# Two windowed attentions in a two-group encoder: a unit's transposes first, then its products with the values in one run; the sample's attention of layer 1 goes quad by quad over both halves

## The chip, the cores and the metric

The kernel runs on one core of a Trainium2 chip. The metric is the device time of one execution in microseconds (us). "Layer 0" is the even layer of the reference, "layer 1" the odd one. "Sample" is the group of 1024 tokens (letter s in names), "prompt" the group of 512 (letter p).

## The reference, cut to what matters

Two groups go through the same two layers with shared weights. Layer 0 has a dense attention and mixture B, a mixture of sliding windows at three dilations over 8 heads. Layer 1 has attention C, a neighbourhood attention on a grid 64 wide with a learned bias over 12 heads, and a Fourier mixer. Each layer is a projection in, the mixers, a gate, a projection out, a norm and a residual. Attention C, cut:

```
def row_block(args):
    r, qr = args
    r0 = jnp.clip(r - kh // 2, 0, rows - kh)
    kr = lax.dynamic_slice_in_dim(kg, r0, kh, axis=1)
    vr = lax.dynamic_slice_in_dim(vg, r0, kh, axis=1)
    bias = rpb[:, row_idx[None, :, None], col_idx[:, None, :]]
    sc = jnp.einsum('bchd,bjkhd->bhcjk', qr, kr) * scale + bias[None]
    sc = jnp.where(col_mask[None, None, :, None, :], sc, NEG_INF)
    p = jax.nn.softmax(sc.reshape(b, h, GRID_W, kh * GRID_W), axis=-1)
    return jnp.einsum('bhcjk,bjkhd->bchd', p, vr)
```

Mixture B is three such softmaxes with windows of 128, 512 and 2048 at dilations 1, 4 and 16, weighted by their sums; the kernel computes them as one softmax.

## The kernel before, in words

Linear layers run on TensorE as three products each of a high and a low part (`mm`, line 143; `tok_gemm`, `chan_gemm`). The names of their outputs tell the job: `t1v` values, `c1k`, `c1q`, `c1g` and `c1d` keys, queries and gates of layer 1, `y` the projection out. The weights come by DMA (`ws...`), are split by ScalarE (`wh...`) and by VectorE or GpSimd (`wl...`). All loads and stores are issued by one queue, that of SyncE (SP), in order; a load whose buffer is still read waits at its head, and all behind it wait too.

**Attention C** (`attn_c_unit`) works in units of one head and one half of the queries (512 of them; the prompt has one half). That makes 24 units for the sample and 12 for the prompt. A unit has four tiles of 128 queries. For each tile: scores on TensorE (`scs` or `scp`), bias and maximum on VectorE (L1096), exponential on ScalarE (L1101), division on VectorE (L1104), three transposes (two for the prompt) into one PSUM tile (`ptcs`, L147), one copy of it to SBUF (`ptccs`, L664, in turn on VectorE and ScalarE), and three (two) products with the values (`ocs`, L670). At the unit's end `fold` (L679, L680) adds the two halves of the output and a DMA stores it (`m1s`).

A product with the values (`pv2`) uses only 64 of the array's columns: `tile_position=(0, 64 * (n % 2))` puts successive products of a unit on the left and the right half by turns, and `fold` adds the halves. Each product of these numbers is two matmul instructions in the trace (288 products of `ocs` are 576 instructions).

**Mixture B** (`attn_b_pair`, `out_b`) works in pairs of heads and one half of the queries. Its scores (`sbs`, `sbp`, lines 800 and 805) use tiles of the array too: eight products of L805, each 64 rows by 32 columns, stand behind two or four of L800. `out_b` then transposes a head's probabilities into four PSUM tiles (`pt1`, `pt2`; three for the prompt), copies each (`ptc1`, `ptc2`) and multiplies with the values (`obs`, `obp`): 14 products for a head of the sample, ten for one of the prompt.

PSUM has two buffers for transposes (TB = 2), one for the output of a unit (OB = 1) and two for scores (SB = 2). The copies have four buffers (tags `pth` and `ptl`, PTB = 2 each), values five (VB = 5).

**Order.** `run` writes the jobs in a list; in layer 1 of the sample it is u0, then k, q, v for each of three quads of heads, then g0, g1, g2 and d0. Attention C of a quad is called behind the job of its values. A scheduler in the framework then decides at build time how the instructions of different calls are interleaved on each engine; on the chip each engine takes its list in order. After the last job, `s3` projects the prompt's output (`y`), and `s3_two` the sample's. Their left operand is made by `s3_operand`: for each of eight blocks two loads (`og` from `m1` and `g1`), a product with the gate (L890, on GpSimd or VectorE), a cast (`hhm`, L891, ScalarE) and a difference (`hlm`, L892, VectorE). The blocks go through three buffers (tag `sp`, SPB = 3), which the gates' outputs (`gt1d`) use as well.

Of the kernel before, what the change touches and what calls it, by code (L numbers as in the profile page):

```python
# [18 lines left out]
P = 128  # L19
D = 1024  # L20
KC = D // P
HD = 64
# [100 lines left out]
class Body:  # L123
# [537 lines left out]
    def copy_pt(self, pt, nm, w=512, rows=P):  # L661
        self.np += 1
        t = self.sb.tile([P, 512], F32, tag="pt" + "hl"[self.np % 2], name="ptc" + nm, bufs=PTB)
        (self.nc.vector.tensor_copy if self.np % PTD == 0 else self.nc.scalar.copy)(t[:rows, :w], pt[:rows, :w])  # L664
        return t

    def pv2(self, out, v, p, n):

        x = 64 * (n % 2)
        self.nc.tensor.matmul(out[x:x + HD], v, p, start=n < 2, stop=False, tile_position=(0, x), skip_group_check=True)  # L670

    def fold(self, po, nm, w=512, view=None):

# [147 lines left out]
    def out_b(self, g, h, pr, x, ev, V1, V2, nm):  # L821
        hf = g.hf
        po = self.pO(f"o{nm}")

        for gi in range(2):
            pt = self.pT(f"pt1{nm}{gi}")
            for i, (t, j) in enumerate(((0, 0), (0, 1), (1, 0), (1, 1))):
                self.tr(pt[:, i * P:(i + 1) * P], ev[2 * gi + t][:, j * P:(j + 1) * P])
            ph = self.copy_pt(pt, f"1{nm}{gi}")
            for j, t, cnt, b in ((0, 0, 1, 0), (1, 0, 2, 1), (2, 1, 1, 3)):  # L830
                t += 2 * gi
                self.pv2(po[:, t * P:(t + cnt) * P], V1[2 * gi + j], ph[:, b * P:(b + cnt) * P], j if gi == 0 else 2 + j)

        pc = po.rearrange("p (t r a) -> p r t a", t=4, r=4)
        for kt in range(hf):
            pt = self.pT(f"pt2{nm}{kt}")
            for t in range(4):
                self.tr(pt[:, t * P:(t + 1) * P], ev[t][:, 256 + kt * P:256 + (kt + 1) * P])
            p2 = self.copy_pt(pt, f"2{nm}{kt}").rearrange("p (t r a) -> p r t a", t=4, r=4)
            for r in range(4):  # L840
                self.pv2(pc[:, r], V2[r * hf + kt], p2[:, r], 2 + r)
        of = self.fold(po, nm, view=lambda v: v.rearrange("p (t r a) -> p r t a", t=4, r=4))
        self.dma(self.md[0, g.name, pr][HD * x:HD * x + HD, 512 * h:512 * h + 512], of)

# [204 lines left out]
    def attn_c_unit(self, g, h, head):  # L1049

        nc, pool = self.nc, self.sb
        n, S, nh = g.name, g.S, g.nhalf
        nrow = 12 if nh == 2 else 8
        NG = nrow // 4
# [26 lines left out]
        for kind, wo, w in ((0, 8, 24), (1, 0, 32), (2, 0, 24)):  # L1081
            b = self.l1.tile([P, nrow, w], F32, tag="bias", name=f"bi{nm}{kind}", bufs=BB)
            nc.gpsimd.tensor_add(b, T[:, :, wo:wo + w], self.mcol[:, kind, wo:wo + w].unsqueeze(1).to_broadcast([P, nrow, w]))  # L1083
            bias[kind] = b
        po = self.pO("o" + nm)
        k3 = km.rearrange("p (r c) -> p r c", c=GRID)
        for i in range(4):
            c0, c1 = max(16 * i - 8, 0), min(16 * i + 24, GRID)
            w = c1 - c0
            W, kw = nrow * w, 4 * w  # L1090
            b = bias[(0, 1, 1, 2)[i]]
            e = pool.tile([P, 1024], F32, tag="e", name=f"e{nm}{i}", bufs=EB)[:, 0:W]
            ps = self.pS(f"s{nm}{i}")[:, 0:W]
            self.qk(ps.rearrange("p (r c) -> p r c", c=w), q, slice(P * i, P * i + P), k3[:, :, c0:c1])
            m = pool.tile([P, 1], F32, tag="nmax", name=f"m{nm}{i}", bufs=4)
            nc.vector.tensor_tensor_reduce(out=e, in0=ps, in1=b.rearrange("p r w -> p (r w)"), scale=1.0,  # L1096
                                           scalar=-3.0e38, op0=ALU.add, op1=ALU.max, accum_out=m)
            ngm = pool.tile([P, 1], F32, tag="nmx2", name=f"ngm{nm}{i}", bufs=4)
# [9 lines left out]
            ph = self.copy_pt(pt, f"{nm}{i}", NG * P, kw)  # L1108
            for x in range(NG):
                self.pv2(po[:, i * P:(i + 1) * P], Vs[i][:kw, x], ph[:kw, x * P:(x + 1) * P], NG * i + x)  # L1110
        self.dma(self.md[1, n, pr][HD * hh:HD * hh + HD, 512 * h:512 * h + 512], self.fold(po, nm))


# [111 lines left out]
    def run(self):  # L1225
# [85 lines left out]
        with tc.tile_pool(name="l1", bufs=1) as self.l1:  # L1311
# [30 lines left out]
            for n, kind in enumerate(jobs):  # L1342
# [7 lines left out]
                if n == FS[1]:  # L1350
                    third(*four)
                    for q in range(3):
                        self.attn_c(gp, 0, q)
                elif kind[0] == "v":
                    self.attn_c(gs, 0, int(kind[1]))
                    if kind == "v2":
                        for q in range(3):
                            self.attn_c(gs, 1, q)
# [41 lines left out]
```

## Time and profile before

| | |
|---|---|
| median of 3 runs | 1936.8 us (1934.24 to 1936.91) |
| the profiled execution | 1936.24 us, of which span of the instructions 1934.2 us |
| busy share of the span | TensorE 96%, VectorE 62%, ScalarE 48%, GpSimd 31% |
| mean granted clock of TensorE | 0.988 |
| DMA | 333 MB, 172 GB/s |

The span runs from the first to the last instruction; the profiled execution is 2.0 us longer than its span. Times in the rows below are us from the span's start. A matmul's end is modelled, so the distance of two starts is the better measure of what one costs.

### The profile page before, as it was taken

The numbers are of one execution on the slowest core, as the hardware profiler recorded it, in microseconds if no ns is written. First come the engines' busy times: TensorE is split into PE (matmuls) and PEld (weight loads), VectorE is DVE, ScalarE is ACT, GpSimd is POOL, SyncE is SP. The second block draws the span as 40 slices with busy tenths as digits, with TensorE's granted clock in tenths as the row PEclk, the third lists the DMA queues.
The fourth block names the chain that finished last, engine by engine and source line by source line (L and its number), as shares of the span: only waits on it lengthen the run. The fifth ranks groups of instructions, "written<-read, shape, count | busy, mean of one in ns | idle before, by whom it ended". The sixth has DMA issues, their size and how long they took to land. (4 is left out here: it accounts for less than half of the span.)

```text
span 1934.2 us, 37850 instructions
## 1 busy us (share of the span) xinstructions
PE 1857.0 (96%) x13752; PEld 1614.9 (83%) x13752; DVE 1195.3 (62%) x3110; ACT 927.1 (48%) x2197; POOL 591.4 (31%) x534
## 2 busy tenths in 40 slices
PE   6999999999999999999999989799999999998998
PEld 4789768999998988889977667788887888887898
DVE  2688863254767666767765677564566544668733
ACT  3456543343356554555554555453554433445531
POOL 3631224354722121121101121353433323335310
PEclk9999999999999999999999999899999999999999
DMA  9754445467763323244344563654677664668643
GB/s 303 253 175 147 126 138 184 126 197 224 231 207 112 104 93 108 64 135 145 116 146 150 182 193 113 205 181 136 216 233 224 195 180 150 200 206 267 221 156 142
DMA packets 255353, 333.03 MB, mean 172 GB/s; under 512 B 25672, under 2 KB 172456, under 8 KB 255168
## 3 DMA queue, kind: packets, MB, share of 16 engines
q1 hardware_dynamic: 255168, 330.62, 54.4%
q8 instruction: 108, 1.77, 0.4%
q14 instruction: 77, 0.63, 0.1%
HBM read 248.68 MB, written 81.87 MB: 171 GB/s over the span
## 5 line engine op out<-in xcount | busy, mean ns | idle before, releaser
L143 PE MATMUL y<-who,hhm 128*128 128x256 f32 x768 | 219.9, 288 | 13.0 <-ACT hhm L891 13.0
L143 PE MATMUL y<-who,hlm 128*128 128x256 f32 x768 | 218.6, 288 | 2.9 <-DVE hlm L892 2.9
L143 PE MATMUL y<-wlo,hhm 128*128 128x256 f32 x768 | 218.6, 287 | 0.2 <-DVE wlo L386 0.2
L143 PEld LDWEIGHTS y<-who,hhm 128*128 128x128 f32 x768 | 148.1, 193 | 16.6 <-ACT hhm L891 14.1
L143 PEld LDWEIGHTS y<-who,hlm 128*128 128x128 f32 x768 | 147.6, 193 | 5.4 <-DVE hlm L892 3.9
L143 PEld LDWEIGHTS y<-wlo,hhm 128*128 128x128 f32 x768 | 148.2, 194 | 1.8 <-issue 1.4
L717 ACT ACTIVATE eas<-sas,nmas 128x512 f32<-128x512 f32 x128 | 86.8, 684 | 69.9 <-DVE nmas L713 69.6
L1083 POOL TENSOR_TENSOR bics<-TTcs,mkc 128x288 f32<-128x288 f32 (+1 forms) x72 | 65.5, 911 | 127.7 <-DVE mcs L1096 108.1
L654 DVE TENSOR_TENSOR ptlas<-ptas,pthas 128x512 fp32r<-128x512 f32 x128 | 85.7, 685 | 19.6 <-ACT pthas L652 18.8
L386 POOL TENSOR_TENSOR wlo<-wso,who 128x512 fp32r<-128x512 f32 x40 | 55.9, 1400 | 132.4 <-ACT who L385 106.5
L708 DVE TENSOR_REDUCE mxas<-sas 128x1 f32<-128x512 f32 x128 | 86.3, 683 | 12.7 <-PE sas L143 12.2
L652 ACT CAST pthas<-ptas 128x512 fp32r<-128x512 f32 x128 | 70.5, 590 | 29.1 <-PE ptas L147 25.7
L143 PE MATMUL t1v<-wh1v,hh 128*128 128x256 f32 x288 | 82.2, 286 | 0.0
L143 PE MATMUL t1v<-wh1v,hl 128*128 128x256 f32 x288 | 82.0, 285 | 0.0
L143 PE MATMUL t1v<-wl1v,hh 128*128 128x256 f32 x288 | 81.9, 285 | 0.0
L1101 ACT ACTIVATE ecs<-ecs,ngmcs 128x288 f32<-128x288 f32 (+1 forms) x96 | 54.8, 571 | 56.3 <-DVE ngmcs L1099 54.8
L914 ACT ACTIVATE ysq<-y 128x256 f32<-128x256 f32 x96 | 36.6, 382 | 87.7 <-PE y L143 70.6
L147 PE MATMUL ptas<-ident,eas 128*128 128x128 f32 x512 | 76.6, 273 | 0.3 <-DVE eas L725 0.3
L143 PE MATMUL oas<-pthas,Vas 128*128 128x256 f32 x256 | 68.9, 285 | 0.0
L143 PE MATMUL oas<-ptlas,Vas 128*128 128x256 f32 x256 | 68.5, 294 | 0.2 <-DVE ptlas L654 0.2
L891 ACT CAST hhm<-og 128x512 fp32r<-128x512 f32 x48 | 29.7, 619 | 75.4 <-POOL og L890 46.1
L385 ACT CAST who<-wso 128x512 fp32r<-128x512 f32 x80 | 48.7, 616 | 35.3 <-PE y L143 10.8
(628 smaller groups left out, 6317.2 us busy)
## 6 DMA issues: line engine op xcount, KB each, us to landing
wso<-w_out_ab SPq DMA_DIRECT2D x48, 256.0 KB
kcs<-k1s SPq DMA_DIRECT2D x24, 384.0 KB
wso<-w_out_cd SPq DMA_DIRECT2D x32, 256.0 KB
ws1k<-w_in_cd SPq DMA_DIRECT2D x28, 256.0 KB
wskb<-w_in_ab SPq DMA_DIRECT2D x24, 256.0 KB
wsqb<-w_in_ab SPq DMA_DIRECT2D x24, 256.0 KB
wsvb<-w_in_ab SPq DMA_DIRECT2D x24, 256.0 KB
ws1q<-w_in_cd SPq DMA_DIRECT2D x24, 256.0 KB
```

Of the source, the lines that this page charges most:

```text
L143: self.nc.tensor.matmul(out, l, r, start=start, stop=stop, skip_group_check=True)
L147: self.nc.tensor.transpose(out, in_, self.ident[:k, :k])
L385: nc.scalar.copy(hi, st)
L386: (nc.vector if c in dve else nc.gpsimd).tensor_sub(lo, st, hi)
L652: nc.scalar.copy(h[:rows, :w], pt[:rows, :w])
L654: nc.vector.tensor_sub(lo[:rows, :w], pt[:rows, :w], h[:rows, :w])
L708: nc.vector.tensor_reduce(mx[:, c:c + 1], ps, op=ALU.max, axis=AX.X, negate=True)
L717: nc.scalar.activation(e[:, 512 * c:512 * c + 512], pss[c], AF.Exp, bias=nmx, accum_out=den[:, c:c + 1])
L891: nc.scalar.copy(hh, t)
L914: nc.scalar.activation(sq[:, 0:256], ps[:, t], AF.Square, accum_out=ss[j][:, job:job + 1])
L1083: nc.gpsimd.tensor_add(b, T[:, :, wo:wo + w], self.mcol[:, kind, wo:wo + w].unsqueeze(1).to_broadcast([P, nrow, w]))
L1101: nc.scalar.activation(e, e, AF.Exp, bias=ngm, scale=0.125, accum_out=den)
```

## The change

In a unit of attention C and in a head of mixture B, all transposes and their copies now come first, and the products with the values follow in one run. `together` makes the first product wait for the last copy and ties each product to the one before it on TensorE, so that the scheduler cannot put anything between them. In layer 1, the second half of the sample's queries is no longer called after the last job of values for all three quads together: each quad's job of values is followed by both halves of that quad. The number of instructions of each kind stays.

```
@@ -661,13 +661,20 @@
     def copy_pt(self, pt, nm, w=512, rows=P):
         self.np += 1
         t = self.sb.tile([P, 512], F32, tag="pt" + "hl"[self.np % 2], name="ptc" + nm, bufs=PTB)
-        (self.nc.vector.tensor_copy if self.np % PTD == 0 else self.nc.scalar.copy)(t[:rows, :w], pt[:rows, :w])
+        self.copied = (self.nc.vector.tensor_copy if self.np % PTD == 0 else self.nc.scalar.copy)(t[:rows, :w], pt[:rows, :w])
         return t
 
+    def together(self, ms):
+
+        self.after(ms[0], self.copied)
+        for a, b in zip(ms, ms[1:]):
+            self.after(b, a, False)
+
     def pv2(self, out, v, p, n):
 
         x = 64 * (n % 2)
-        self.nc.tensor.matmul(out[x:x + HD], v, p, start=n < 2, stop=False, tile_position=(0, x), skip_group_check=True)
+        return self.nc.tensor.matmul(out[x:x + HD], v, p, start=n < 2, stop=False, tile_position=(0, x),
+                                     skip_group_check=True)
 
     def fold(self, po, nm, w=512, view=None):
 
@@ -822,23 +829,28 @@
         hf = g.hf
         po = self.pO(f"o{nm}")
 
+        p1, p2, ms = [], [], []
         for gi in range(2):
             pt = self.pT(f"pt1{nm}{gi}")
             for i, (t, j) in enumerate(((0, 0), (0, 1), (1, 0), (1, 1))):
                 self.tr(pt[:, i * P:(i + 1) * P], ev[2 * gi + t][:, j * P:(j + 1) * P])
-            ph = self.copy_pt(pt, f"1{nm}{gi}")
-            for j, t, cnt, b in ((0, 0, 1, 0), (1, 0, 2, 1), (2, 1, 1, 3)):
-                t += 2 * gi
-                self.pv2(po[:, t * P:(t + cnt) * P], V1[2 * gi + j], ph[:, b * P:(b + cnt) * P], j if gi == 0 else 2 + j)
+            p1.append(self.copy_pt(pt, f"1{nm}{gi}"))
 
         pc = po.rearrange("p (t r a) -> p r t a", t=4, r=4)
         for kt in range(hf):
             pt = self.pT(f"pt2{nm}{kt}")
             for t in range(4):
                 self.tr(pt[:, t * P:(t + 1) * P], ev[t][:, 256 + kt * P:256 + (kt + 1) * P])
-            p2 = self.copy_pt(pt, f"2{nm}{kt}").rearrange("p (t r a) -> p r t a", t=4, r=4)
+            p2.append(self.copy_pt(pt, f"2{nm}{kt}").rearrange("p (t r a) -> p r t a", t=4, r=4))
+        for gi in range(2):
+            for j, t, cnt, b in ((0, 0, 1, 0), (1, 0, 2, 1), (2, 1, 1, 3)):
+                t += 2 * gi
+                ms.append(self.pv2(po[:, t * P:(t + cnt) * P], V1[2 * gi + j], p1[gi][:, b * P:(b + cnt) * P],
+                                   j if gi == 0 else 2 + j))
+        for kt in range(hf):
             for r in range(4):
-                self.pv2(pc[:, r], V2[r * hf + kt], p2[:, r], 2 + r)
+                ms.append(self.pv2(pc[:, r], V2[r * hf + kt], p2[kt][:, r], 2 + r))
+        self.together(ms)
         of = self.fold(po, nm, view=lambda v: v.rearrange("p (t r a) -> p r t a", t=4, r=4))
         self.dma(self.md[0, g.name, pr][HD * x:HD * x + HD, 512 * h:512 * h + 512], of)
 
@@ -1083,6 +1095,7 @@
             nc.gpsimd.tensor_add(b, T[:, :, wo:wo + w], self.mcol[:, kind, wo:wo + w].unsqueeze(1).to_broadcast([P, nrow, w]))
             bias[kind] = b
         po = self.pO("o" + nm)
+        pts, ms = [], []
         k3 = km.rearrange("p (r c) -> p r c", c=GRID)
         for i in range(4):
             c0, c1 = max(16 * i - 8, 0), min(16 * i + 24, GRID)
@@ -1105,9 +1118,11 @@
             pt = self.pT(f"pt{nm}{i}")
             for x in range(NG):
                 self.tr(pt[:kw, x * P:(x + 1) * P], e[:, x * kw:(x + 1) * kw])
-            ph = self.copy_pt(pt, f"{nm}{i}", NG * P, kw)
+            pts.append((self.copy_pt(pt, f"{nm}{i}", NG * P, kw), kw))
+        for i, (ph, kw) in enumerate(pts):
             for x in range(NG):
-                self.pv2(po[:, i * P:(i + 1) * P], Vs[i][:kw, x], ph[:kw, x * P:(x + 1) * P], NG * i + x)
+                ms.append(self.pv2(po[:, i * P:(i + 1) * P], Vs[i][:kw, x], ph[:kw, x * P:(x + 1) * P], NG * i + x))
+        self.together(ms)
         self.dma(self.md[1, n, pr][HD * hh:HD * hh + HD, 512 * h:512 * h + 512], self.fold(po, nm))
 
 
@@ -1352,10 +1367,8 @@
                     for q in range(3):
                         self.attn_c(gp, 0, q)
                 elif kind[0] == "v":
-                    self.attn_c(gs, 0, int(kind[1]))
-                    if kind == "v2":
-                        for q in range(3):
-                            self.attn_c(gs, 1, q)
+                    for h in range(2):
+                        self.attn_c(gs, h, int(kind[1]))
             _, H = self.s3(1, 2, H=ops[0], last=lambda: self.s3_operand(1, 0))
             self.wend = ([(("wh", "wl"), WB)] * WB + [(("wxh", "wxl"), WX)] * WX + [(("qh", "ql"), QB)] * QB +
                          [(("pth", "ptl"), PTB)] * PTB + [(("V", "V"), VB)] * (VB // 2))
```

What this does to the order, first on TensorE in attention C of the sample. These are the rows of the unit of head 4, second half (`41` in the names; the last digit is the tile of queries, x3 says three in a row). Before:

```order
L147 MATMUL ptcs412_21722<-ident_63,ecs412_21709 128x128 x2
L670 MATMUL ocs41_21664<-ptccs410_21682,Vcs410_21648 64x128 x3
L670 MATMUL ocs41_21664<-ptccs411_21704,Vcs411_21650 64x128 x3
L147 MATMUL ptcs412_21722<-ident_63,ecs412_21709 128x128
L147 MATMUL ptcs413_21744<-ident_63,ecs413_21731 96x128 x3
...
L670 MATMUL ocs41_21664<-ptccs412_21726,Vcs412_21652 64x128 x3
L670 MATMUL ocs41_21664<-ptccs413_21748,Vcs413_21654 64x128 x3
L147 MATMUL ptcs510_21787<-ident_63,ecs510_21774 96x128 x3
```

The unit's 12 products stand in two runs of six, with transposes on both sides of each. After:

```order
L147 MATMUL ptcs510_20819<-ident_63,ecs510_20806 96x128 x3
L143 MATMUL t1v211_21587<-wh1v200_21406,hh110_16601 128x256
L676 MATMUL ocs41_20696<-ptccs410_20714,Vcs410_20680 64x128 x3
L676 MATMUL ocs41_20696<-ptccs411_20733,Vcs411_20682 64x128 x3
L676 MATMUL ocs41_20696<-ptccs412_20752,Vcs412_20684 64x128 x3
L676 MATMUL ocs41_20696<-ptccs413_20771,Vcs413_20686 64x128 x3
L147 MATMUL ptcs511_20838<-ident_63,ecs511_20825 128x128 x3
```

The 12 products stand in one run, and one tile of the next unit's transposes (`ptcs510`) was moved ahead of it.

Second, on TensorE in mixture B of the sample, at the scores of one tile of queries (`sbs711`). Before:

```order
L147 MATMUL pt2bs6110_12638<-ident_63,ebs6110_12445 128x128 x2
L147 MATMUL pt2bs6110_12638<-ident_63,ebs6111_12447 128x128 x2
L800 MATMUL sbs7110_12712<-kbs71_12664,qbs71_12666 128x256
L800 MATMUL sbs7111_12713<-kbs71_12664,qbs71_12666 128x256
L805 MATMUL sbs7110_12712<-kbs71_12664,qbs71_12666 32x256
L805 MATMUL sbs7111_12713<-kbs71_12664,qbs71_12666 32x256
L805 MATMUL sbs7110_12712<-kbs71_12664,qbs71_12666 32x256
L805 MATMUL sbs7111_12713<-kbs71_12664,qbs71_12666 32x256
L805 MATMUL sbs7110_12712<-kbs71_12664,qbs71_12666 32x256
L805 MATMUL sbs7111_12713<-kbs71_12664,qbs71_12666 32x256
L805 MATMUL sbs7110_12712<-kbs71_12664,qbs71_12666 32x256
L805 MATMUL sbs7111_12713<-kbs71_12664,qbs71_12666 32x256
```

The two rows with 128 in front are L800's, the eight with 32 are L805's, in one group. After:

```order
L147 MATMUL pt1bs6111_12625<-ident_63,ebs6111_12447 128x128 x4
L807 MATMUL sbs7110_12712<-kbs71_12664,qbs71_12666 128x256
L807 MATMUL sbs7111_12713<-kbs71_12664,qbs71_12666 128x256
L812 MATMUL sbs7110_12712<-kbs71_12664,qbs71_12666 32x256
L147 MATMUL pt2bs6110_12632<-ident_63,ebs6110_12445 128x128 x2
L147 MATMUL pt2bs6110_12632<-ident_63,ebs6111_12447 128x128 x2
L812 MATMUL sbs7111_12713<-kbs71_12664,qbs71_12666 32x256
L812 MATMUL sbs7110_12712<-kbs71_12664,qbs71_12666 32x256
L812 MATMUL sbs7111_12713<-kbs71_12664,qbs71_12666 32x256
L812 MATMUL sbs7110_12712<-kbs71_12664,qbs71_12666 32x256
L812 MATMUL sbs7111_12713<-kbs71_12664,qbs71_12666 32x256
L812 MATMUL sbs7110_12712<-kbs71_12664,qbs71_12666 32x256
```

A group of transposes now stands behind the first of the eight.

Third, on SyncE's queue, where the operand of the prompt's projection out begins to load (`og120` and on). Before:

```order
L140 DMA og120_23048<-m1p0_174 128x512
L140 DMA og120_23048<-g1p00_166 128x512
L140 DMA g1s07_117<-gt1d001_23042 128x512
L140 DMA og121_23054<-m1p1_175 128x512
L140 DMA og121_23054<-g1p01_167 128x512
L140 DMA m1s2_128<-ofcs41_21753 64x512
```

There the store of head 4's output (`ofcs41`) stands between the loads of the first blocks; the stores of 16 of the 24 units stand ahead of the first load. After:

```order
L140 DMA g1s06_116<-gt1d000_23013 128x512
L140 DMA og120_23048<-m1p0_174 128x512
L140 DMA m1s5_131<-ofcs111_22540 64x512
L140 DMA og120_23048<-g1p00_166 128x512
L140 DMA g1s07_117<-gt1d001_23042 128x512
L140 DMA og121_23054<-m1p1_175 128x512
L140 DMA og121_23054<-g1p01_167 128x512
```

Now the store of the last unit of attention C (`ofcs111`) stands between the two loads of the first block, and all other blocks come behind it. On TensorE 53 matmuls of `c1d` stand between that unit's products and the first `y`, and no attention stands among the `y`; before, 18 of the 24 units had begun their products when the first `y` came, and attention was mixed with `y` up to the last.

## Rows read from the trace of the kernel before

**Rows 1.** The page, busy us of each engine (share of the span) and instructions.

```profile
PE 1857.0 (96%) x13752; PEld 1614.9 (83%) x13752; DVE 1195.3 (62%) x3110; ACT 927.1 (48%) x2197; POOL 591.4 (31%) x534
```

**Rows 2.** Windows: length, busy us by engine (count), granted clock, DMA share, GB/s.

```profile
1480.00:1500.00 20.00, 18.03 (x158) 16.28 (x157) 13.96 (x49) 9.67 (x25) 7.92 (x9) 1.00 0.78 225
1660.00:1680.00 20.00, 20.00 (x136) 16.34 (x136) 12.37 (x39) 9.69 (x24) 9.01 (x9) 1.00 0.70 209
1740.00:1760.00 20.00, 15.58 (x96) 12.00 (x95) 17.33 (x41) 9.84 (x22) 11.78 (x10) 0.83 0.92 266
1760.00:1780.00 20.00, 19.11 (x170) 17.92 (x168) 15.35 (x44) 11.81 (x34) 9.58 (x10) 1.00 0.79 252
1780.00:1800.00 20.00, 18.45 (x152) 16.62 (x152) 19.81 (x56) 11.88 (x33) 10.31 (x8) 1.00 0.79 251
1800.00:1820.00 20.00, 16.69 (x143) 15.18 (x143) 12.10 (x32) 10.07 (x26) 5.07 (x4) 0.91 0.61 203
```

**Rows 3.** What TensorE waited for from 1740 to 1820: us, times, longest.

```profile
PE ocs L670 <- ACT ptccs L664: 3.3, 1, 3.3
```

**Rows 4.** Timeline of TensorE, products with the values: start, us, engine, instruction, count.

```profile
1386.68 0.44 PE L670 MATMUL ocp<-ptccp,Vcp 128*64 128x128 f32 x4
1387.05 0.42 PE L147 MATMUL ptcp<-ident,ecp 128*96 128x128 f32 x2
...
1486.66 1.31 PE L670 MATMUL ocs<-ptccs,Vcs 96*64 96x128 f32 x18
1487.90 0.86 PE L147 MATMUL ptcs<-ident,ecs 128*96 128x128 f32 x6
...
1493.84 0.65 PE L670 MATMUL ocs<-ptccs,Vcs 96*64 96x128 f32 x6
1494.42 0.88 PE L147 MATMUL ptcs<-ident,ecs 128*128 128x128 f32 x6
...
1665.35 0.40 PE L143 MATMUL c1g<-hh,wh1g 128*128 128x512 f32 x1
1665.58 0.40 PE L143 MATMUL c1g<-hl,wh1g 128*128 128x512 f32 x1
1665.90 0.88 PE L670 MATMUL ocs<-ptccs,Vcs 128*64 128x128 f32 x12
1666.71 0.86 PE L147 MATMUL ptcs<-ident,ecs 128*96 128x128 f32 x6
1667.33 0.38 PE L143 MATMUL scs<-kcs,qhcs 128*128 128x288 f32 x1
```

**Rows 5.** Timeline of TensorE, scores of mixture B, whole and cut in two.

```profile
1098.62 0.66 PE L805 MATMUL sbs<-kbs,qbs 64*32 64x256 f32 x16
1099.22 0.66 PE L147 MATMUL pt2bs<-ident,ebs 128*128 128x128 f32 x4
...
1104.14 0.64 PE L805 MATMUL sbs<-kbs,qbs 64*32 64x256 f32 x8
1104.70 0.66 PE L670 MATMUL obs<-ptc2bs,V2bs 128*64 128x128 f32 x8
1105.29 0.64 PE L805 MATMUL sbs<-kbs,qbs 64*32 64x256 f32 x8
1105.86 0.39 PE L143 MATMUL y<-who,hlm 128*128 128x256 f32 x1
```

**Rows 6.** Timeline of SyncE and of VectorE: an operand made without attention beside it.

```profile
1851.08 0.32 SPq L140 DMA_DIRECT2D og<-m1s  x1
...
1850.36 0.69 DVE L892 TENSOR_TENSOR hlm<-og,hhm 128x512 fp32r<-128x512 f32 x1
...
1856.66 0.69 DVE L892 TENSOR_TENSOR hlm<-og,hhm 128x512 fp32r<-128x512 f32 x1 [0.69 <-ACT hhm L891]
...
1861.12 0.68 DVE L892 TENSOR_TENSOR hlm<-og,hhm 128x512 fp32r<-128x512 f32 x1
```

**Rows 7.** Timeline of VectorE: one copy of transposes in mixture B.

```profile
1213.24 0.69 DVE L664 COPY ptc1bs<-pt1bs 128x512 f32<-128x512 f32 x1
```

More of the change, by code (lines that the diff above doesn't have):

```diff
@@ L663, in copy_pt, with together @@
         t = self.sb.tile([P, 512], F32, tag="pt" + "hl"[self.np % 2], name="ptc" + nm, bufs=PTB)
-        (self.nc.vector.tensor_copy if self.np % PTD == 0 else self.nc.scalar.copy)(t[:rows, :w], pt[:rows, :w])
+        self.copied = (self.nc.vector.tensor_copy if self.np % PTD == 0 else self.nc.scalar.copy)(t[:rows, :w], pt[:rows, :w])
         return t
+    def together(self, ms):
+        self.after(ms[0], self.copied)
+        for a, b in zip(ms, ms[1:]):
+            self.after(b, a, False)
     def pv2(self, out, v, p, n):
         x = 64 * (n % 2)
-        self.nc.tensor.matmul(out[x:x + HD], v, p, start=n < 2, stop=False, tile_position=(0, x), skip_group_check=True)
+        return self.nc.tensor.matmul(out[x:x + HD], v, p, start=n < 2, stop=False, tile_position=(0, x),
+                                     skip_group_check=True)
     def fold(self, po, nm, w=512, view=None):
@@ L823, in out_b @@
         po = self.pO(f"o{nm}")
+        p1, p2, ms = [], [], []
         for gi in range(2):
@@ L828, in out_b @@
                 self.tr(pt[:, i * P:(i + 1) * P], ev[2 * gi + t][:, j * P:(j + 1) * P])
[L829 to L832, printed above, removed]
+            p1.append(self.copy_pt(pt, f"1{nm}{gi}"))
         pc = po.rearrange("p (t r a) -> p r t a", t=4, r=4)
@@ L838, in out_b @@
                 self.tr(pt[:, t * P:(t + 1) * P], ev[t][:, 256 + kt * P:256 + (kt + 1) * P])
-            p2 = self.copy_pt(pt, f"2{nm}{kt}").rearrange("p (t r a) -> p r t a", t=4, r=4)
+            p2.append(self.copy_pt(pt, f"2{nm}{kt}").rearrange("p (t r a) -> p r t a", t=4, r=4))
+        for gi in range(2):
+            for j, t, cnt, b in ((0, 0, 1, 0), (1, 0, 2, 1), (2, 1, 1, 3)):
+                t += 2 * gi
+                ms.append(self.pv2(po[:, t * P:(t + cnt) * P], V1[2 * gi + j], p1[gi][:, b * P:(b + cnt) * P],
+                                   j if gi == 0 else 2 + j))
+        for kt in range(hf):
             for r in range(4):
-                self.pv2(pc[:, r], V2[r * hf + kt], p2[:, r], 2 + r)
+                ms.append(self.pv2(pc[:, r], V2[r * hf + kt], p2[kt][:, r], 2 + r))
+        self.together(ms)
         of = self.fold(po, nm, view=lambda v: v.rearrange("p (t r a) -> p r t a", t=4, r=4))
@@ L1085, in attn_c_unit @@
         po = self.pO("o" + nm)
+        pts, ms = [], []
         k3 = km.rearrange("p (r c) -> p r c", c=GRID)
@@ L1107, in attn_c_unit @@
                 self.tr(pt[:kw, x * P:(x + 1) * P], e[:, x * kw:(x + 1) * kw])
-            ph = self.copy_pt(pt, f"{nm}{i}", NG * P, kw)
+            pts.append((self.copy_pt(pt, f"{nm}{i}", NG * P, kw), kw))
+        for i, (ph, kw) in enumerate(pts):
             for x in range(NG):
-                self.pv2(po[:, i * P:(i + 1) * P], Vs[i][:kw, x], ph[:kw, x * P:(x + 1) * P], NG * i + x)
+                ms.append(self.pv2(po[:, i * P:(i + 1) * P], Vs[i][:kw, x], ph[:kw, x * P:(x + 1) * P], NG * i + x))
+        self.together(ms)
         self.dma(self.md[1, n, pr][HD * hh:HD * hh + HD, 512 * h:512 * h + 512], self.fold(po, nm))
@@ L1354, in run @@
                 elif kind[0] == "v":
[L1355 to L1358, printed above, removed]
+                    for h in range(2):
+                        self.attn_c(gs, h, int(kind[1]))
             _, H = self.s3(1, 2, H=ops[0], last=lambda: self.s3_operand(1, 0))
```

## The prediction

> **What bounds the kernel now.** I read the page first: TensorE is busy 96% of the span, VectorE 62%, ScalarE 48% [rows 1]. So time is won by making TensorE's own list shorter, or by filling its few gaps. Then windows of 20 us through layer 1 [rows 2], one for each kind of stage. The reader is to see three. At 1660 to 1680 TensorE has no gap and VectorE is busy for 12.37 of 20: here a shorter list is worth all that it saves. At 1480 to 1500, where attention C units follow closely among the values' job, TensorE is idle for 1.97. At 1740 to 1820, where the last units stand among the first products of the projection out, it is idle for 4.42 + 0.89 + 1.55 + 3.31 = 10.2, VectorE is busy for up to 19.81 of 20, and the granted clock falls to 0.83 and 0.91. The list of waits says what one part of that was: a run of products that waited 3.3 for ScalarE's copy of its transposes [rows 3]. Last the timeline, for what one instruction costs in its company, by the distance of two starts.
>
> **The change part by part.** The sum is made against the profiled execution, 1936.2, which lies 0.6 below the median of the three runs, so I make no correction for it.
>
> *Fewer runs of products with the values.* Starts in [rows 4] give 0.37 for a run of 4 matmuls (1386.68 to 1387.05), 0.58 for 6, 0.81 for 12 and 1.24 for 18. Two products stand beside each other on the halves of the array, so count slots: a pair of products takes two (two matmuls deep), and an odd product at the end takes two alone. 4, 6, 12 and 18 matmuls are then 2, 4, 6 and 10 slots. (1.24 − 0.37) / 8 = 0.11 a slot, and 0.37 − 2 × 0.11 = 0.15 for the run itself; this gives 0.59 and 0.81 for the other two, as measured. To that comes what its neighbour loses: two `c1g` start 0.23 apart, but the last one ahead of a run takes 0.32, so 0.09 on entering. What leaving costs stands in no row; it lies between nothing and the same 0.09, and I take 0.05. Together 0.29 a run.
>
> Runs are counted in the order of the two kernels: 51 of `ocs` become 24, 30 of `ocp` become 12, 40 of `obs` 16 and 16 of `obp` 9. That is 137 to 61, and 76 × 0.29 = 22.0. 18 runs of `ocs` had an odd number of products and now have twelve: one slot each, 18 × 0.11 = 2.0. So **−24.0**.
>
> *Scores of mixture B are cut more often.* The scheduler now puts other work into groups of L805: the pieces rise from 35 to 46 for the sample (19 stay 19 for the prompt). [Rows 5] show a whole group of two tiles, 0.60 (1098.62 to 1099.22), and one cut into two eights, 0.56 and 0.57. A cut costs 0.56 + 0.57 − 0.60 = 0.53, and entering and leaving 0.14 more as above. 11 × 0.67 = **+7.3**.
>
> There is another way to count these two edits. The rows price a run by its length and a split score group by its own pair. The Trainium skill, in "TensorEngine Tiling (Array Packing)", section Tiling Modes (Key Properties), says that changing the tiling mode drains the engine, while changing the tile within a mode does not. Counted so, the changes of mode fall by 133 between the two orders, and at 0.145 each (half of a run's 0.29, an estimate) that is 19.3 saved, where the rows give 16.7: the total would be 1915. The trace agrees that a change costs something, the 0.32 against 0.23 above; that it is one price whatever the neighbours are, no row shows. I keep the rows' sum.
>
> *Attention leaves the `y`.* With both halves of a quad behind its values, all 24 units are done before the first `y`; 53 `c1d` stand between. The gaps of 1740 to 1820 have their cause in VectorE, which does bias, maximum, division and half of the copies for the last units and at the same time `hlm`, weights and the copies out for `y`. The 10.2 of idle would go. The clock there would be back too: means of 0.83 and 0.91 over 20 us are 6.8 + 3.6 = 10.4 us at the lower level (1.2 of 2.4 GHz). Half of that is lost if TensorE is busy all the time, 5.2, and at its busy share of four fifths, 4.2; I take 4.5. Together **−14.7**. The units themselves go to the stages of k, q and g, where [rows 2] show room (1660 to 1680), which is why their work is not charged again.
>
> *The operand of the projection out comes late.* This is what takes the place of the stall. SyncE's queue is one list: before, `og120` stood behind 16 units' stores; now its second load stands behind the store of the last unit, `ofcs111`, and seven more blocks queue behind that. The store can be issued when `fold` is done, an estimated 2 after the unit's last product. What a block then takes is shown where the sample's operand is made without attention [rows 6]: 1851.08 to 1856.66 from issue to `hlm` is 5.6, and five blocks take 1861.12 − 1850.36 = 10.8, 2.15 each. The eighth block is there at 2 + 5.6 + 7 × 2.15 = 22.6 behind the last product. TensorE has 53 `c1d` of 0.23, 12.2, and then seven blocks' three products each of the first `y`; these have 256 columns, half of `c1g`'s 512, so 0.12 each: 14.7 in all. It would stand for up to 7.9. The first blocks share three buffers and can load beside each other, which the pace of 2.15 (behind stores and loads of weights) does not count. I take 6 of stall, and by the ratio above (4.5 of clock for 10.2 idle) 2.5 of clock: **+8.5**, with the bounds 0 and the whole 14.7 given back.
>
> *End of layer 0.* The last head of mixture B now has to finish all copies before its first product: one copy of 0.69 [rows 7], four transposes, and a second copy's wait are in the chain where before they were beside products. I take **+1.5**; that the chain is otherwise shorter by the last runs bounds it by −3, three copies more that nothing covers by +5 in the other direction.
>
> *New waits in the dense stages.* A first product that waits for the fourth copy holds all of TensorE's list behind it: the next unit's transposes, the values' or keys' products, and by those the next scores. Cover is one tile of the next unit and matmuls of `t1v` that the scheduler moved ahead; if that cover is gone, the wait is one copy and its semaphore. There are 24 units, in the stages where before 12 stood. Bounds: nothing, and 1.97 (the idle of 1480 to 1500, two and a half units) for each of 12 pairs, 23.6. TensorE hides most of it in 1660 to 1680, so I lean to the lower end: **+3.0**.
>
> 1936.2 − 24.0 + 7.3 − 14.7 + 8.5 + 1.5 + 3.0 = 1917.8, so **1918**.
>
> **The rivals.** What can be told from no change here is about 0.2%, 3.9 us: faster is below 1932.9, slower above 1940.7.
>
> *The gain comes whole.* The blocks load while `c1d` runs, and nothing stands: 1917.8 − 8.5 = 1909.3, and 1904.8 if the small waits vanish too. For it: `c1d` is 12.2 long and DMA is free of attention's stores by then. Against it: the order of SyncE's queue, and 5.6 for one block.
>
> *VectorE and ScalarE set the pace.* What TensorE saves in runs becomes waits for copies and divisions, since those remain as many: 16.7 of net saving gone, 1917.8 + 16.7 = 1934.5, no change. For it: VectorE is busy 19.81 of 20 at 1780 to 1800. Against it: at 1660 to 1680 it has 7.6 of 20 free while TensorE has none. Half of this effect gives 1926. The Trainium skill's "TensorEngine Tiling (Array Packing)", section Performance Considerations (PSUM Bottleneck), has this rule: tiling speeds up TensorE, but not the emptying of PSUM, which may then become the limit. In 1780 to 1800 the trace agrees (19.81), in 1660 to 1680 not (12.37).
>
> *A unit starts late (the other side).* With a quad's two halves back to back, the units' V, q and k loads, whose buffers come free only when the longer, later run of products ends, reach the head of SyncE's queue too late, and loads of weights wait behind them. Its place is the three stages of values and those behind them. Without the term of new waits the sum is 1914.8; 24 units that each wait w give 1914.8 + 24 w. From w = 1.07 on the kernel is slower than 1940.7; at 1.97, what one such pair waits now, it is 1962. For it: DMA is busy 0.78 at 1480 to 1500 and 0.92 at 1740 to 1760. Against it: at 1660 to 1680, with units beside `c1g`, it is 0.70 and TensorE loses nothing; and five V buffers hold more than one unit's values.
>
> That the change does not do what it says I exclude: the order shows each sample unit's 12 products in one run.
>
> **How the numbers follow.** The forecast's own case, 1912 to 1924: 0.50. The gain whole, 1904 to 1912: 0.20. Half of it lost to copies, 1924 to 1932.9: 0.15. All net saving of the runs lost, no change: 0.07. Units late, slower: 0.08. Faster is 0.50 + 0.20 + 0.15 = 0.85. The low end, 1904, is the sum with the first three terms alone (1936.2 − 24.0 + 7.3 − 14.7 = 1904.8). The high end, 1932, leaves out the last two cases, 0.15.
>
> **What the profile after would show.** Right, if distances of starts give about 1.5 for a run of twelve products and there are 24 of `ocs`; if the stage of the last `c1d` and first `y` has the clock at 1.00 but for one gap of some 6 before or in the first `y`, ended by `hlm`; and if the stages of values keep their idle of 2 in 20. Wrong, if runs of `ocs` wait for their copies again and again (an idle column beside `ocs` in the sum by lines of more than 10), if the gap at `y` is absent or over 12, or if TensorE's busy time falls by much less than 17 while its idle stays: then the price of a run was wrong.

## The result, and the profile after

The changed kernel takes 1950.65 us (median of 4 runs, 1946.81 to 1952.99), the one before beside it 1935.52 (1933.06 to 1936.91): a ratio of 1.0078, 95% interval 1.0055 to 1.0100. It is slower by 15 us. The forecast was 1918, with 1904 to 1932, and the direction was wrong. The profiled execution has a span of 1950.8 and a granted clock of 0.979.

The page's busy times, which answer to [rows 1]:

```profile
PE 1854.3 (95%) x13752; PEld 1626.5 (83%) x13752; DVE 1197.3 (61%) x3110; ACT 926.3 (47%) x2197; POOL 591.9 (30%) x534
```

TensorE does the same instructions and is busy 2.7 us less, where I had taken 17 off its list. Its idle time rises from 77.2 to 96.4. The busy time hides a gain, because more of it lies at the lower level of the clock: 62.3 us, before 32.2. Two `y` start 0.213 apart there and 0.120 at the full level, so 13.1 of the 30.1 more are the clock's (an estimate), and without them TensorE would be busy 15.8 less. Its waits for the whole span, longest sum first:

```profile
PE y L143 <- ACT hhm L903: 21.2, 7, 10.3
PE xt L147 <- DVE x L318: 9.8, 2, 8.8
PE ocs L676 <- DMA Vcs<-v1s: 7.3, 7, 1.7
PE y L143 <- DVE hlm L904: 5.1, 6, 2.3
...
PE sbs L807 <- DVE ebs L880: 3.1, 1, 3.1
PE sbs L807 <- DVE rdbs L879: 2.9, 1, 2.9
PE obs L676 <- DVE ptc2bs L664: 2.8, 2, 2.0
```

The reader is to see a new line, products that wait for values (`Vcs`), seven times, and a longer first line, `y` that waits for its operand. In the kernel before that line was

```profile
PE y L143 <- ACT hhm L891: 13.0, 5, 10.0
```

and there was none with `Vcs`. The 10.3 in the longer one is the end of layer 0, which before had too (10.0). Windows of the stages that answer to [rows 2], columns as there:

```profile
1496.00:1516.00 20.00, 17.82 (x148) 16.57 (x147) 12.11 (x45) 8.67 (x24) 6.24 (x8) 0.92 0.66 205
...
1656.00:1676.00 20.00, 20.00 (x135) 16.34 (x133) 12.39 (x42) 8.18 (x23) 5.90 (x7) 1.00 0.68 209
...
1776.00:1796.00 20.00, 13.73 (x58) 10.98 (x57) 14.39 (x16) 8.32 (x14) 8.09 (x6) 0.75 0.75 243
1796.00:1816.00 20.00, 20.00 (x156) 20.00 (x156) 9.81 (x14) 7.83 (x20) 7.91 (x6) 0.91 0.77 248
```

Among the gates attention C still costs no idle. At 1776 to 1796, where no attention is left, TensorE is idle for 6.27 and the clock is at 0.75.

**Where the time came from.** Compare the two traces by the end of the same job. When dense attention of layer 0 ends (last `oas`), the changed kernel is 2.1 us ahead (984.6 against 986.7). When mixture B's last product ends, it is 13.4 behind (1239.5 against 1226.1). At the end it is 16.6 behind. So mixture B's stage loses 15.5, and all that follows, layer 1 with it, from which I expected most of the gain, loses another 3.2.

### The profile page after: what moved, and what is told of

The parts are those of the page before. It is cut to its first block, busy times and chain, and to the rows that moved or that the text cites. A ratio compares the mean times of both kernels' runs of the same rounds, so it can differ in the third digit from the quotient of the medians.

```text
span 1950.8 us, 37884 instructions
## 1 busy us (share of the span) xinstructions
PE 1854.3 (95%) x13752; PEld 1626.5 (83%) x13752; DVE 1197.3 (61%) x3110; ACT 926.3 (47%) x2197; POOL 591.9 (30%) x534
## 4 chain that ended last, share of the span: by engine, by line
PE 41%; DMA 8%; DVE 3%; ACT 1%; issue 1%; POOL 1%; SPq 0%; POOLq 0%; DVEq 0%; ACTq 0%
PE y L143 6%; PE c1g L143 5%; PE c1q L143 5%; PE c1k L143 5%; PE t1v L143 4%; DMA Vcs<-v1s 2%; PE ocs L676 2%; PE ptcs L147 2%; PE obs L676 2%; PE scs L143 1%; PE c1d L143 1%; DMA og<-g1s 1%; PE sbs L812 1%; DMA og<-g0s 1%; PE oas L143 1%; PE sbs L807 1%
## 5 line engine op out<-in xcount | busy, mean ns | idle before, releaser
L143 PE MATMUL y<-who,hhm 128*128 128x256 f32 x768 | 224.5, 294 | 21.2 <-ACT hhm L903 21.2
L143 PEld LDWEIGHTS y<-who,hhm 128*128 128x128 f32 x768 | 152.4, 199 | 24.6 <-ACT hhm L903 23.2
L143 PEld LDWEIGHTS y<-wlo,hhm 128*128 128x128 f32 x768 | 152.2, 199 | 5.5 <-DVE wlo L386 2.2
L902 POOL TENSOR_TENSOR og<-og 128x512 f32<-128x512 f32 x24 | 33.6, 1402 | 125.8 <-DMA og<-g0s 40.9
```

Source lines behind the costliest of these rows:

```text
L143: self.nc.tensor.matmul(out, l, r, start=start, stop=stop, skip_group_check=True)
```

## Experiments

Ratios are to the kernel before, run beside each; all times are medians. "Whole change less mixture B" is attention C grouped and the quads in the new order.

**1 to 4, the parts.** Each kernel is the changed one with the other parts put back: `attn_c_unit` alone, `out_b` alone, the order of the quads alone, and all but `out_b`.

> Only attention C has its products in one run; mixture B's products and the order of the quads are those of before. Two theories of the loss. M: it is made in mixture B, where the changed trace is 17 us later at the end of layer 0 than at its middle against before, while layer 1 comes out even. Q: it is made by the queue of loads in layer 1 (late values, late operand of the projection out), and mixture B's share is a matter of what stands beside it. By my sum the runs of attention C give back 15 us; seven waits for values took 7.3 in the changed kernel, if they belong to the grouping they are here too. Both theories then expect 1920 to 1928; above 1935 the saving of the runs itself is in doubt.

> Only mixture B has its products in one run. M expects 1949 to 1953 (before's 1935.5 and 14 to 17). Q expects 1934 to 1938: 9 us of runs saved against 7 for cut score groups, and no loss of its own.

> Only the order of the quads is changed: both halves behind each quad's values, products as before. The changed trace has 11.8 us of idle and 17 us at half clock around the projection out, the one of before 10.2 and 10.4 there. M expects 1934 to 1941 (the two stalls about even, the values' waits small). Q expects 1945 to 1952.

> The whole change without its part in mixture B. M expects 1932 to 1937 (1950.65 less 14 to 17). Q expects 1945 to 1950, within 5 us of the changed kernel.

| kernel | us | ratio | 95% interval |
|---|---|---|---|
| C alone | 1930.78 | 0.9983 | 0.9970 to 0.9995 |
| mixture B alone | 1954.38 | 1.0101 | 1.0080 to 1.0121 |
| order of the quads alone | 1951.19 | 1.0085 | 1.0064 to 1.0106 |
| whole change less mixture B | 1932.62 | 0.9985 | 0.9970 to 0.9999 |

M holds for the changed kernel: without mixture B's part it is a little faster than before, at the edge of the scatter (the interval ends at 0.9999). Q holds for the order of the quads by itself, which neither theory had beside a harmless mixture: it costs 16 with the old products, and nothing with the grouped ones. C alone gave 3 where 15 had been expected.

**7, mixture B without the tie.** The transposes stay ahead of the products in the code:

```
-        self.together(ms)
         of = self.fold(po, nm, view=...)
```

> Only mixture B changed, all transposes of a head ahead of its products in the code, but without the ties: the order on TensorE shows 42 runs of products again and 41 pieces of score groups instead of 46. If the one run (its wait for the last copy, with all of TensorE's list behind it) makes the loss of 19.7 us, this is 1934 to 1941. If it is the transposes ahead of the products, and what the scheduler puts elsewhere for that, it stays at 1947 to 1955.

1935.71, ratio 0.9995 (0.9981 to 1.0009). The loss is gone, so it comes with the tie, not with the moved transposes. The tie makes the run and its wait, and with it go 5 of the 11 more pieces of score groups. TensorE's waits in mixture B, 1070 to 1232, first with mixture B alone changed:

```profile
PE y L143 <- ACT hhm L903: 5.7, 2, 4.5
PE sbs L807 <- DVE ebs L880: 3.5, 1, 3.5
PE sbs L807 <- DVE rdbs L879: 3.2, 1, 3.2
PE obs L676 <- DVE ptc2bs L664: 2.0, 1, 2.0
```

and without the tie:

```profile
PE y L143 <- ACT hhm L902: 4.0, 2, 3.8
PE pt1bs L147 <- DVE ebs L879: 2.0, 2, 1.4
PE sbs L807 <- DVE wlo L386: 1.2, 1, 1.2
```

The clock fell with the waits. Two windows of the kernel with mixture B alone changed:

```profile
1070.00:1100.00 30.00, 24.65 (x213) 17.25 (x213) 19.50 (x57) 14.22 (x30) 5.12 (x4) 0.87 0.65 204
1100.00:1130.00 30.00, 24.99 (x232) 19.19 (x231) 22.20 (x55) 13.93 (x30) 4.36 (x3) 0.85 0.54 170
```

The same two windows of the kernel before:

```profile
1070.00:1100.00 30.00, 29.14 (x248) 19.39 (x246) 19.28 (x53) 14.09 (x31) 3.86 (x4) 1.00 0.57 187
1100.00:1130.00 30.00, 25.39 (x231) 19.83 (x232) 23.60 (x58) 14.40 (x31) 5.11 (x4) 0.94 0.72 222
```

**8, one key.** The keys of the sample's mixture B are loaded for the first pair of heads only:

```
-        km = pool.tile([P, S], F32, tag="k", ...)
-        self.dma(km, self.kd[0, n, pr])
+        if g.idx == 0 or (h == 0 and pr == 4):
+            self.kb = pool.tile([P, S], F32, tag="k", ...)
+            self.dma(self.kb, self.kd[0, n, pr])
+        km = self.kb
```

> Only mixture B changed, as in the kernel that has its part alone, and the keys of the sample's mixture B loaded once for the first pair of heads (7 loads are left out, so the output is not the mixture's). There scores waited 7.1 us at three changes of pair for keys whose only buffer comes free late, with the clock at the lower level after each. If that is the loss, 1938 to 1944. If the loss is made by the copies, the operand of the projection out and the cut score groups, 1949 to 1955.

1952.51, ratio 1.0090 (1.0069 to 1.0111). The keys are not it. `y` waited 2.1, 4.8 and 4.6 for operands instead.

**9, 13 and 14, the operand of the filler.** In the changed kernel's trace this chain stands behind the products of one head. Timelines of TensorE, SyncE, GpSimd and ScalarE, in this order:

```profile
1213.52 1.09 PE L676 MATMUL obs<-ptc1bs,V1bs 128*64 128x128 f32 x12
1214.44 1.04 PE L676 MATMUL obs<-ptc2bs,V2bs 128*64 128x128 f32 x16
1215.41 0.64 PE L812 MATMUL sbs<-kbs,qbs 64*32 64x256 f32 x8
...
1221.61 0.49 PE L147 MATMUL pt2bs<-ident,ebs 128*128 128x128 f32 x3
1226.64 0.80 PE L143 MATMUL y<-who,hhm 128*128 128x256 f32 x2 [4.54 <-ACT hhm L903]
```

```profile
1218.15 0.50 SPq L140 DMA_DIRECT2D m0s<-ofbs  x1
1221.06 0.34 SPq L140 DMA_DIRECT2D og<-m0s  x1
```

```profile
1224.67 1.26 POOL L902 TENSOR_TENSOR og<-og 128x512 f32<-128x512 f32 x1 [11.27 <-DMA og<-m0s]
```

```profile
1225.97 0.62 ACT L903 CAST hhm<-og 128x512 fp32r<-128x512 f32 x1 [2.68 <-POOL og L902]
```

The head's last product is over at 1215.4. Its output is stored at 1218.15, loaded again as `og` at 1221.06, multiplied, cast, and is there at 1226.6, 11.2 later. TensorE came to the `y` that reads it at 1222.1, 6.7 behind the products, and waited 4.54. In between stood 31 `y` of older blocks. The kernel before has the same chain (TensorE, SyncE, ScalarE and TensorE again):

```profile
1199.65 0.66 PE L670 MATMUL obs<-ptc2bs,V2bs 128*64 128x128 f32 x8
1205.87 0.35 SPq L140 DMA_DIRECT2D og<-m0s  x1
1210.04 0.62 ACT L891 CAST hhm<-og 128x512 fp32r<-128x512 f32 x1
1211.14 0.40 PE L143 MATMUL y<-who,hhm 128*128 128x256 f32 x2
```

It took about as long, 10.4 from the last product (over at 1200.24) to the end of the cast, but 63 `y` stood in between and nothing waited. To take that dependence away, blocks 4 to 7 of the operand are made from the gate alone, here and in the kernel before:

```
-            self.dma(st[:, 0], self.md[l, n, k][:, us])
+            self.dma(st[:, 0], self.gd[l, n, gu, k] if l == 0 and g.idx and k > 3 else self.md[l, n, k][:, us])
```

> Only mixture B changed, as in the kernel that has its part alone (1954.4), and the sample's projection out of layer 0 no longer reads mixture B's outputs: blocks 4 to 7 of its operand are made from the gate alone (mixture B's output is left out of the result). The products of that projection are the work that TensorE puts between a head's transposes and its products, and they waited for operands made of earlier heads' outputs: 1.2 and 4.5 us in the kernel with its part alone, 2.1, 4.8 and 4.6 in the one with one key. If that dependence, head to operand to filler, makes the loss, 1938 to 1946. If it is copies and cut groups alone, 1950 to 1955.

> The control to the kernel with mixture B grouped and a free operand (1927.7): the kernel before, with blocks 4 to 7 of the sample's operand in layer 0 made from the gate alone (mixture B's output is left out of the result). In the trace of before the end of layer 0 waits 10.0 us for this operand, with 10.2 us at the lower clock behind it, so 1918 to 1922 here. Theory D, that grouping in mixture B loses only by the chain from head to operand to filler: then the grouped kernel with a free operand should not be slower than this one, within 3. If keys, copies and cut groups cost something of their own, this one is 5 to 10 faster than 1927.7.

> Mixture B grouped, with the free operand and the one key together (mixture B's output and 7 key loads are left out). With the free operand scores still waited 3.3 and 2.0 us at changes of pair. If keys make what is left of the loss, 1919 to 1923; if copies and cut groups do, 1926 to 1930.

| kernel | us | ratio | 95% interval |
|---|---|---|---|
| mixture B grouped, free operand | 1927.74 | 0.9955 | 0.9940 to 0.9970 |
| before, free operand | 1921.42 | 0.9928 | 0.9911 to 0.9945 |
| grouped, free operand, one key | 1926.20 | 0.9955 | 0.9941 to 0.9969 |

With the operand as it is, grouping costs 19.7; with a free operand it costs 6.3 (1927.74 less 1921.42, barely outside the scatter). So some 13 of it come by the dependence of the filler on the heads. Kernel 9 fell below its range because the edit also takes away the wait at the end of layer 0, with grouping or without; the control shows that share, 13.6. The 13 are not the waits alone: the scheduler, once free, also puts more `y` ahead of mixture B's last product (109 more in the grouped kernel, 50 more in the other), and no run tells waits and order apart. Keys give 1.5 at most of the rest, which is within scatter. The rest is not idle time: from the last product of dense attention to the first `ocs` both traces with a free operand idle for 12.0. In the grouped one `sbs` takes 4.6 more there, idle left out, and `obs` only 0.5 less; the whole stretch is 3.3 longer. So in these traces what is left lies in the cut score groups, not in waits for copies.

**5 and 10, the operand of layer 1.** In the changed kernel SyncE did what the prediction said:

```profile
1765.87 0.37 SPq L140 DMA_DIRECT2D og<-m1p  x1
1771.29 0.45 SPq L140 DMA_DIRECT2D m1s<-ofcs  x1
1771.79 0.58 SPq L140 DMA_DIRECT2D og<-g1p  x1
```

The second load of the first block came 5.9 behind the first, at the last unit's store. One kernel issues the operand's loads from GpSimd's queue, the other gives four blocks other buffers:

```
+            eng = nc.gpsimd if l == 1 and u == 2 else None
-            self.dma(st[:, 0], self.md[l, n, k][:, us])
+            self.dma(st[:, 0], self.md[l, n, k][:, us], eng)
```

```
+            if l == 1 and u == 2 and 3 <= k < 7:
+                st = pool.tile([P, 1024], F32, tag="e", ...).rearrange("p (t c) -> p t c", t=2)
+            else:
                 st = pool.tile([P, 2, 512], F32, tag="sp", ...)
```

> The change without its part in mixture B (1932.6 before), and the 16 loads of the prompt's operand in layer 1 issued from GpSimd's queue instead of SyncE's, where they stood behind the store of the last unit. TensorE's list stays as it was but for a few rows. In that kernel the first products of the projection out waited 6.9 us in five pieces, and the clock stood 10.2 us at the lower level there. If the place in the queue is what makes the operand late, most of it goes: 1919 to 1925. If the operand is bound by its buffers or by VectorE and ScalarE, the waits stay: 1929 to 1934.

> The change without its part in mixture B (1932.6), with four of the eight blocks of the prompt's operand in layer 1 loaded into the buffers of the finished attention (tag e) instead of the three that they share. TensorE's list differs in a few rows. A block there takes some 6.4 us from issue to free, and three buffers give one each 2.1. If the buffers bind, the 6.9 us of waits and most of 10.2 at the lower clock go: 1920 to 1926. If VectorE, ScalarE and the operand's own buffers bind, 1930 to 1934, as with the other queue.

The other queue gave 1934.18, ratio 0.9996 (0.9984 to 1.0007): nothing. It is no clean test of the place in the queue, since GpSimd's own product for the first block then stood behind its third load, which waited for a buffer, and the first `hhm` came no earlier. The buffers gave 1920.65, ratio 0.9926 (0.9903 to 0.9949). What `y` waited for from 1750 to 1810, first without, then with them:

```profile
PE y L143 <- ACT hhm L898: 4.7, 3, 2.1
PE y L143 <- DVE hlm L899: 2.2, 2, 1.1
```

```profile
PE y L143 <- DVE wlo L386: 1.3, 1, 1.3
PE y L143 <- DVE hlm L902: 0.9, 1, 0.9
```

6.9 of waits for the operand become 0.9, and with the clock it is 12.0 us (10.7 between the two traces, from the last `ocs` to the end). So the three shared buffers make the operand late. How, is not shown: with four more, four whole blocks are loaded ahead of the store of the last unit (from 1736.80, the store at 1753.81), where half a block was, and for the rest SyncE waits 1.2 us for an `hlm` to free a buffer instead of 3.7. No run tells the earlier place from the faster pace.

**6, 11 and 15, the values.** How the seven waits look in the changed kernel:

```profile
1521.93 1.53 PE L676 MATMUL ocs<-ptccs,Vcs 96*64 96x128 f32 x24
...
1530.39 0.88 PE L676 MATMUL ocs<-ptccs,Vcs 96*64 96x128 f32 x12
1531.69 0.65 PE L676 MATMUL ocs<-ptccs,Vcs 128*64 128x128 f32 x6 [0.42 <-DMA Vcs<-v1s]
1533.47 0.65 PE L676 MATMUL ocs<-ptccs,Vcs 96*64 96x128 f32 x6 [1.13 <-DMA Vcs<-v1s]
```

A run without waits stands at 1521.93, the second head of a pair. At 1530.39 the next pair begins and stops twice in the middle of its run. Kernel 6 loads values once; 11 puts a pair's fourth tile of values into a buffer of its own (six in all); 15 does that with the old order of the quads and mixture B as before:

```
-        if hh == 0:
+        if hh == 0 and (g.idx == 0 or (head == 0 and h == 0)):
```

```
-                V = pool.tile([P, NG, P], F32, tag="V", ..., bufs=VB)
+                V = (self.l1.tile([P, NG, P], F32, tag="V3", ..., bufs=1) if nh == 2 and i == 3 else
+                     pool.tile([P, NG, P], F32, tag="V", ..., bufs=VB))
```

> The change without its part in mixture B, and the values of the sample's attention C loaded once for the first pair of heads and used for all (44 loads of values are left out, so the output is not attention's). In that kernel seven runs of products waited 6.4 us for values, with 3.4 us at the lower clock. If late values are the price of the run, 1922 to 1927. If they only stand in front of another wait (scores, copies), 1930 to 1934.

> The change without its part in mixture B, with the fourth tile of values of each pair of heads in a sixth buffer: two of the next pair's four tiles can be loaded ahead instead of one. TensorE's list is the same row for row. Without any reload the waits were worth 9. If the buffers make the waits, half of that: 1926 to 1930. If it is the transfers themselves, 1931 to 1935.

> Attention C grouped, mixture B and the order of the quads as before, with the sixth buffer of values. The kernel without it (1930.8) waited 7.3 us for values. If the late values ate the saving of the runs there too, 1918 to 1924, and the order of the quads is then worth 5 at most. If the saving needs the other order, 1928 to 1932.

| kernel | us | ratio | 95% interval |
|---|---|---|---|
| whole change less B, one load of values | 1923.52 | 0.9941 | 0.9927 to 0.9954 |
| whole change less B, six buffers | 1918.99 | 0.9925 | 0.9906 to 0.9945 |
| C alone, six buffers | 1924.26 | 0.9949 | 0.9931 to 0.9968 |

From 1480 to 1760 the products' wait, without and with the sixth buffer, TensorE's list being the same:

```profile
PE ocs L676 <- DMA Vcs<-v1s: 5.5, 6, 1.3
```

```profile
PE ocs L676 <- DMA Vcs<-v1s: 0.2, 1, 0.2
```

The medians differ by 13.6, twice what was expected of the buffer and more than leaving the loads out gave, 9.1. Part of that is scatter: of the 13.9 between the two traces 6.4 lie ahead of the first `ocs` (1490.4 and 1484.0), where the buffer does nothing yet. From the first `ocs` to the last it is 8.7, and 11.5 and 11.1 where the same buffer is added to kernel 10 and, in kernel 16, to the whole change. I put the buffer at 9 to 11. It is 6.5 with the old order of the quads (1930.78 to 1924.26). With values in time, the new order of the quads is worth 5.3 (1924.26 to 1918.99), but the intervals overlap.

**12 and 16, together.** Both edits in the whole change less mixture B, and in the whole change.

> Both of these together. If each binds by its buffers, the gains add: 1914 to 1922, below both kernels. If neither does, 1930 to 1935.

> The whole change, mixture B's part too, with the sixth buffer of values and the operand in the attention's buffers. If the three costs are independent (mixture B 17, values 7 to 13, operand 12), 1912.3 and 17: 1926 to 1932. If mixture B's part hurts only through what it delays in layer 1, 1912 to 1918.

1912.32, ratio 0.9879 (0.9864 to 0.9894), without mixture B's part, and 1927.77, ratio 0.9966 (0.9955 to 0.9978), with it. The first is the fastest kernel of the study, 23 us below before. The gains do not add in full: 12.0 and 13.6 alone, 20.3 together (1932.62 to 1912.32). The stage of the last `c1d` and first `y` in it, 20 us each:

```profile
1740.00:1760.00 20.00, 17.88 (x105) 14.76 (x105) 10.75 (x15) 8.90 (x16) 6.08 (x5) 1.00 0.54 164
1760.00:1780.00 20.00, 20.00 (x170) 20.00 (x169) 10.94 (x18) 7.99 (x22) 7.62 (x6) 1.00 0.89 287
1780.00:1800.00 20.00, 17.38 (x146) 17.17 (x145) 11.42 (x16) 9.35 (x25) 7.58 (x6) 1.00 0.65 211
```

The clock stays at 1.00 where it was 0.75. Mixture B's price, 15.5 between the two, adds to the rest.

## Why the prediction was wrong, step by step

- **Price of a run: right.** The run of 24 matmuls in the changed kernel takes 1.46 (starts 1756.26 and 1757.72):

```profile
1756.26 1.53 PE L676 MATMUL ocs<-ptccs,Vcs 96*64 96x128 f32 x24
1757.72 0.55 PE L147 MATMUL ptcs<-ident,ecs 128*128 128x128 f32 x3
```

  0.15 + 12 × 0.11 gives 1.47. In mixture B a head's 28 matmuls take 1.89 in one run, and took 2.04 in two and 2.19 in three: 0.15 a run again. All `ocs` together, from each start to the next, take 46.3 before (3.3 of it the wait of [rows 3]), 45.6 in the changed kernel and 35.7 with six buffers of values: the waits for values ate what the runs saved. With idle time left out, `ocs`, `ocp` and their transposes take 15.5 less without mixture B's part than before, where the sum has 45 × 0.29 + 2.0 = 15.1. My own sign for a wrong price, a busy time that falls by much less than 17, came true (2.7), but the sign was wrong: it forgot that the clock stretches busy time. The other way of counting, one price for each change of mode, does not fit: a run saved is worth 0.15 by its own length, a cut score group 0.53.
- **Cut score groups: right.** The pieces of `sbs` from L812 take 27.7 where those from L805 took 21.2: 6.5, of which the sum had 11 × 0.53 = 5.8 (the other 1.5 of its 7.3 are neighbours, which these pieces do not hold).
- **End of layer 0, +1.5: this step failed, with the whole of mixture B.** I gave mixture B 31 fewer runs of 0.29, 9.0, less 7.3 for the cuts, and 1.5 for a longer last chain: −0.2. It is +15.5 to +19.7. The sum has no term for waits inside mixture B's stage; it put them at nothing without a reason. I looked at the end of the layer alone, but a head's output is the operand of the work beside it, all through the stage. The tie holds a head's output back to the last copy, while the `y` that could have filled the time is spent ahead of the run. [Rows 7] and the bounds of −3 to +5 say nothing of that.
- **New waits in the dense stages, +3.0: the place was right and the size wrong.** The rival of the late unit had the mechanism: values whose buffers come free only when the run ends. I argued against it that five buffers hold more than one unit's values. They hold one pair's four tiles and one of the next, and the run needs all four at once. It cost 9 to 11, within the bound of 23.6, where I had 3.0.
- **The operand of the projection out, +8.5: the stall right, pace and clock not.** The stall is 6.27 at 1776 to 1796 where I took 6. That is luck in part: I took 2 us off because three buffers let blocks load beside each other, and the blocks came slower than the 2.15 each of [rows 6], 2.69 (`hlm` from 1776.88 to 1795.71); the eighth was there 25.9 behind the last product and not 22.6. With the clock it cost 10.2 to 12.0, within the bound of 14.7; the clock's share, 2.5, was too small, and the clock fell to 0.75 where I expected 1.00 but for one gap.
- **Attention leaves the `y`, −14.7: in kind as said.** The waits of [rows 3] are gone, and the kernel with both buffers keeps the clock at 1.00 there. The changed kernel traded them for the operand's. The size is not shown: from attention C alone with six buffers of values to that kernel it is 11.9 (1924.26 to 1912.32), with the operand's buffers in it, which the old order was not given.
- **VectorE sets the pace: did not decide.** The edits that freed most changed buffers, not VectorE's work. No run made VectorE's work less, so a smaller share of it is not excluded.

The ledger of the miss, 1950.65 − 1917.8 = 32.9, along the kernels that take one cause away after the other: values and operand 11.4 (both edits together give 22.9, 1950.65 to 1927.77, and I had 3.0 + 8.5 for them), mixture B 15.7 (15.5 and 0.2). The other 5.8 are terms that were to gain and gained less (1912.32, where the sum has 1906.5 when these costs are left out: 1917.8 − 11.5 + 0.2); which of them, no run shows.

**What stays open.** Why the order of the quads costs 16 with the old products and nothing with the grouped ones: its trace has waits for queries of 1.6, 1.9 and 2.2 that the grouped one lacks, but no run separated them. Neither set of buffers was tried in the kernel before, so it is not shown how much of the 23 us they would give there; its trace has no wait for values.

## What to carry to other kernels

Work tied into one run saves its switches, here just as the rows said, but it moves every result of the run to its end and every operand to its start: ask of each operand whether all of it can be there at once (buffers for the next unit, not for this one), and of each result who waits for it and what stands between. A cost found at one wait ("the end of the layer") should be looked for in every place where the same chain runs. When a good change measures slow, take its parts apart before giving it up: two of these three, with a buffer here and there, are 23 us faster.

## What the runs showed of the hardware

Most of the larger waits had a stretch at the lower level of TensorE's clock beside them or right behind them (in the changed kernel eight waits of 2.2 to 10.3 us), so that a wait costs more than its idle: at 1776 to 1796 of the changed kernel 6.27 of idle stands beside a granted clock of 0.75, and removing 6.0 of waits by the operand's buffers gave 12.0 us by the medians and 10.7 between the traces. Over the whole span the changed kernel has 83.0 us at the lower level, the one before 44.8. A `y` behind another takes 0.213 there and 0.120 at the full level, not quite twice. I had counted 2.5 for the clock.
